# A row softmax over 16384 rows: larger blocks, one broadcast multiply for each, and tiles of twice the size in half as many buffers

## Chip, cores and metric

The kernel runs on one core of one Trainium2 chip. The metric is the device time of one execution in microseconds (us). The median of ten runs of the kernel before is 163.21 us (163.10 to 163.46).

## What is computed

A softmax over the last axis of a float32 tensor of 16 x 1024 x 512, with a temperature of 0.5, so that every element is doubled first:

```python
def reference(x: np.ndarray) -> np.ndarray:
    temp = 0.5
    x_scaled = x / temp
    x_max = np.max(x_scaled, axis=-1, keepdims=True)
    exp_x = np.exp(x_scaled - x_max)
    return (exp_x / np.sum(exp_x, axis=-1, keepdims=True)).astype(np.float32)
```

Input and output are 33.55 MB each. Every byte is read from HBM once and written once.

## The kernel before

The 16384 rows are cut into 8 tiles of 2048 rows. A tile lies on 128 partitions with G = 16 rows of 512 elements each, 32 KiB a partition, and those 16 rows are contiguous in HBM. There are six buffers for tiles, 192 KiB a partition. A tile is transformed in place and stored from where it lies.

A tile is worked on in blocks of B = 4 rows a partition, 32 blocks in all. Five small functions each record one step of a block:

- `shift(i)` on VectorE: the negated maximum of each row (L65, one tensor_reduce for four rows) and its doubling, which is the bias (L67).
- `exponentials(i)` on ScalarE: one activation a row (L74), exp(2x + bias), which also leaves the sum of the row.
- `scale_vector(i)` on VectorE: the reciprocals of the four sums (L87), and three of the four rows multiplied by them, one instruction a row (L89).
- `scale_scalar(i)` on ScalarE: the fourth row multiplied, as a copy with a scale (L95).
- `store(i)` on ScalarE's DMA queue: after the last block of a tile, the whole tile of 4.2 MB (L102).

`load(c)` issues a tile's load on SP's DMA queue (L59). The first tile comes in two pieces, four rows and twelve, the others whole. From the seventh tile on, a load has to wait until the store of the tile six before it has left the buffer.

The order of the instructions on each engine is the order in which the program records them; the schedule is written by hand (`manual_schedule`). The main loop (L105 to L116) is a software pipeline: in step i it records shift and exponentials of block i, then scale_vector of block i-1, scale_scalar of block i-2 and store of block i-3. So on ScalarE the exponentials of block i come ahead of the copy of block i-2. Waits between engines are put in by the framework where data demand them. Each engine, and each DMA queue, works through its own list in order.

Of the kernel before, what the change touches and what calls it, by code (L numbers as in the profile page):

```python
# [1 line left out]

# [4 lines left out]


@with_exitstack
def kernel(  # L10
    ctx: ExitStack,
    tc: tile.TileContext,
    x: bass.AP,
    out: bass.AP,
):
    nc = tc.nc
    fp32 = mybir.dt.float32
    P = nc.NUM_PARTITIONS
    AX = mybir.AxisListType.X
    EXP = mybir.ActivationFunctionType.Exp  # L20
    COPY = mybir.ActivationFunctionType.Copy
    MAX = mybir.AluOpType.max

    D = x.shape[-1]
    xf = x.flatten_outer_dims()
    of = out.flatten_outer_dims()
    N = xf.shape[0]

    G = 16
    B = 4
    N_ACT = 1
    C = N // (P * G)
    assert C * P * G == N
    xr = xf.rearrange("(c p g) d -> c p g d", p=P, g=G)
    outr = of.rearrange("(c p g) d -> c p g d", p=P, g=G)

    FIRST = [(0, 4), (4, 16)]  # L40

    data = ctx.enter_context(tc.tile_pool(name="data", bufs=6))
    stats = ctx.enter_context(tc.tile_pool(name="stats", bufs=6))

    ctx.enter_context(tc.manual_schedule())


    warm = stats.tile([P, 1], fp32, name="warm", bufs=1)
    nc.vector.memset(warm, 0.0)  # L49
    nc.scalar.activation(out=warm, in_=warm, func=EXP)  # L50

    tiles = {}
    blocks = [(c, b) for c in range(C) for b in range(0, G, B)]
    state = {}

    def load(c):
        xt = tiles[c] = data.tile([P, G, D], fp32, name="xt")
        for lo, hi in FIRST if c == 0 else [(0, G)]:
            nc.sync.dma_start(out=xt[:, lo:hi, :], in_=xr[c][:, lo:hi, :])  # L59

    def shift(i):
        c, b = blocks[i]
        xb = tiles[c][:, b : b + B, :]
        negmax = stats.tile([P, B], fp32, name="negmax")
        nc.vector.tensor_reduce(negmax, xb, axis=AX, op=MAX, negate=True)  # L65
        bias = stats.tile([P, B], fp32, name="bias")
        nc.vector.tensor_scalar_mul(bias, negmax, 2.0)  # L67
        state[i] = (xb, bias)

    def exponentials(i):  # L70
        xb, bias = state[i]
        sums = stats.tile([P, B], fp32, name="sums")
        for g in range(B):
            nc.scalar.activation(  # L74
                out=xb[:, g, :],
                in_=xb[:, g, :],
                func=EXP,
                bias=bias[:, g : g + 1],
                scale=2.0,
                accum_out=sums[:, g : g + 1],  # L80
            )
        state[i] = (xb, sums)

    def scale_vector(i):
        xb, sums = state[i]
        recip = stats.tile([P, B], fp32, name="recip")
        nc.vector.reciprocal(recip, sums)  # L87
        for g in range(B - N_ACT):
            nc.vector.tensor_scalar_mul(xb[:, g, :], xb[:, g, :], recip[:, g : g + 1])  # L89
        state[i] = (xb, recip)  # L90

    def scale_scalar(i):
        xb, recip = state[i]
        for g in range(B - N_ACT, B):
            nc.scalar.activation(  # L95
                out=xb[:, g, :], in_=xb[:, g, :], func=COPY, scale=recip[:, g : g + 1]
            )

    def store(i):
        c, b = blocks[i]  # L100
        if b + B == G:
            nc.scalar.dma_start(out=outr[c], in_=tiles[c])  # L102

    n = len(blocks)
    for i in range(n + 3):  # L105
        if i < n:
            if blocks[i][1] == 0:
                load(blocks[i][0])
            shift(i)
            exponentials(i)  # L110
        if 1 <= i <= n:
            scale_vector(i - 1)
        if 2 <= i <= n + 1:
            scale_scalar(i - 2)
        if 3 <= i:
            store(i - 3)  # L116


# [1 line left out]
_INS = ['x']  # L120
_OUTS = [((16, 1024, 512), 'float32')]


# [23 lines left out]
```

## Time and profile before

| | before |
|---|---|
| median of 10 runs | 163.21 us |
| the profiled execution | 163.66 us |
| its span in the profile | 161.6 us |
| VectorE busy | 119.7 us (74%), 193 instructions |
| ScalarE busy | 114.8 us (71%), 290 instructions |
| DMA | 67.14 MB, 416 GB/s over the span |

The span runs from the first instruction of the program to the last; the 2.06 us around it are not in the profile. "Busy" is the time in which an engine executes an instruction. The slices of the profile page cut the span into 40 equal parts of 4.04 us; a digit is the busy share in tenths. In a group of instructions, the numbers behind the bar are the total busy time, the mean duration in ns, and the idle time ahead with what ended it. DVE is VectorE, ACT is ScalarE, SPq and ACTq are the DMA queues of SP and ScalarE. In a view of windows the columns are: length, busy time of VectorE, ScalarE and GpSimd with their counts, the clock of TensorE, the busy share of the DMA engines, and GB/s.

### The profile page before, as it was taken

Reading aid. Unit: us, or ns where it says so; the run is one execution under the profiler, and the core shown is the slowest. Engines: PE = TensorE matmul, PEld = TensorE weight load, DVE = VectorE, ACT = ScalarE, POOL = GpSimd, SP = SyncE. Lnnn points to the kernel's source line nnn. Section 1 sums busy time; section 2 is a strip of 40 time slices with the busy share of each in tenths; the row PEclk is TensorE's granted clock in tenths of the full one; section 3 lists DMA queues with packets and bytes.
Section 4 is the critical chain, followed back from the end, with each engine's and each line's share of the span. In section 5 each row is a group of like instructions: output and inputs, shape, how many; then the busy total and the mean of one; then the engine's idle time right before and its main releaser. Section 6 shows DMA issues by size and latency. Waiting matters only on the chain.

```text
span 161.6 us, 563 instructions
## 1 busy us (share of the span) xinstructions
DVE 119.7 (74%) x193; ACT 114.8 (71%) x290; POOL 0.2 (0%) x4
## 2 busy tenths in 40 slices
DVE  0608999999999999999997999099980999630000
ACT  3071799999999998999996999539993499950000
POOL 0000000000000000000000000000000000000000
DMA  5999999999999999999999999999999999999990
GB/s 185 464 422 487 389 438 470 391 438 341 481 414 406 479 422 397 479 422 397 487 408 397 495 406 389 511 397 389 511 397 389 495 414 391 487 414 406 487 406 24
DMA packets 2452, 67.14 MB, mean 416 GB/s; under 512 B 272, under 2 KB 272, under 8 KB 272
## 3 DMA queue, kind: packets, MB, share of 16 engines
q1 hardware_dynamic: 1296, 33.56, 48.9%
q10 hardware_dynamic: 1152, 33.55, 48.1%
q14 instruction: 4, 0.03, 0.0%
HBM read 33.55 MB, written 33.55 MB: 415 GB/s over the span
## 4 chain that ended last, share of the span: by engine, by line
DMA 54%; DVE 31%; ACT 3%; issue 1%; SPq 0%
DMA xt<-in_x_dram 36%; DVE negmax L65 19%; DMA out_dram<-xt 18%; DVE xt L89 9%; ACT xt L74 2%; DVE bias L67 1%; ACT xt L95 1%; DVE recip L87 1%; SPq L59 0%
## 5 line engine op out<-in xcount | busy, mean ns | idle before, releaser
L74 ACT ACTIVATE xt<-xt,bias 128x512 f32<-128x512 f32 x128 | 90.8, 710 | 28.1 <-DVE bias L67 28.1
L65 DVE TENSOR_REDUCE negmax<-xt 128x4 f32<-128x2048 f32 x32 | 73.0, 2281 | 18.9 <-DMA xt<-in_x_dram 18.9
L89 DVE TENSOR_SCALAR xt<-xt,recip 128x512 f32<-128x512 f32 x96 | 40.9, 483 | 1.1
L74 ACT ACTIVATION_READ_ACCUMULATOR xt<-xt,bias 128x1 f32 x128 | 23.9, 187 | 0.0
L95 ACT ACTIVATE xt<-xt,recip 128x512 f32<-128x512 f32 x32 | 22.4, 706 | 0.0
L87 DVE RECIPROCAL recip<-sums 128x4 f32<-128x4 f32 x32 | 5.5, 171 | 1.6 <-ACT xt L74 1.6
L67 DVE TENSOR_SCALAR bias<-negmax 128x4 f32<-128x4 f32 x32 | 5.4, 170 | 1.1
L50 ACT ACT_TABLE_LOAD x1 | 1.3, 1283 | 0.7 <-PEq L131 0.7
L49 DVE MEMSET warm<- 128x1 f32 x1 | 0.1, 59 | 0.8 <-PEq L131 0.8
L50 ACT ACTIVATE warm<-warm 128x1 f32<-128x1 f32 x1 | 0.2, 202 | 0.0
L131 POOL MEMSET const-bfloat16-1.0<- 128x1 bf16 x1 | 0.1, 101 | 0.0
L131 POOL MEMSET const-uint8-127<- 128x1 uint8 x1 | 0.1, 101 | 0.0
L131 POOL MEMSET const-float32-0.0<- 128x1 f32 x1 | 0.1, 98 | 0.2 <-issue 0.2
L131 POOL MEMSET const-float32-1.0<- 128x1 f32 x1 | 0.1, 98 | 0.0
## 6 DMA issues: line engine op xcount, KB each, us to landing
out_dram<-xt ACTq DMA_DIRECT2D x8, 4096.0 KB, 27.3
xt<-in_x_dram SPq DMA_DIRECT2D x7, 4096.0 KB, 46.4
xt<-in_x_dram SPq DMA_DIRECT2D x1, 3072.0 KB, 11.7
xt<-in_x_dram SPq DMA_DIRECT2D x1, 1024.0 KB, 4.8
```

Source lines behind the costliest of these rows:

```text
L49: nc.vector.memset(warm, 0.0)
L50: nc.scalar.activation(out=warm, in_=warm, func=EXP)
L65: nc.vector.tensor_reduce(negmax, xb, axis=AX, op=MAX, negate=True)
L67: nc.vector.tensor_scalar_mul(bias, negmax, 2.0)
L74: nc.scalar.activation(out=xb[:, g, :], in_=xb[:, g, :], func=EXP, bias=bias[:, g : g + 1], scale=2.0, accum_out=sums[:, g : g + 1],)
L87: nc.vector.reciprocal(recip, sums)
L89: nc.vector.tensor_scalar_mul(xb[:, g, :], xb[:, g, :], recip[:, g : g + 1])
L95: nc.scalar.activation(out=xb[:, g, :], in_=xb[:, g, :], func=COPY, scale=recip[:, g : g + 1])
L131: nc = _bacc.Bacc("TRN2", target_bir_lowering=False, num_devices=1)
```

## The change

Tiles are twice as large: 4 tiles of 32 rows a partition (64 KiB, contiguous in HBM) in three buffers, the same 192 KiB. Loads and stores of the second and third tile are whole, 8.4 MB; those of the first and fourth come in halves of 16 rows, and the first half of the first tile is loaded in three pieces of 1, 3 and 12 rows. The fourth tile takes the first one's buffer by name, half by half.

Blocks are of 4, 4, 8 and 16 rows in the first tile, of 16 rows in the second and third, and of 16, 8 and 8 in the fourth: 11 in all. The three multiplies of a block on VectorE, one a row, become one tensor_mul over three quarters of its rows, with the reciprocals broadcast along the 512 elements. ScalarE still copies the last quarter, one row at a time.

The main loop is another: shift(0), shift(1) and exponentials(0) come ahead; then step i records exponentials of block i+1, scale_vector and scale_scalar of block i, shift of block i+2, and store of block i. So on ScalarE the copies and the store of block i come after the exponentials of block i+1.

The diff, cut to its core (line numbers of the new kernel that the text speaks of: loads L72, maximum L80, doubling L84, exponentials L91, reciprocals L106, multiply L108, copies L117, stores L125):

```diff
-    G = 16
-    B = 4
-    N_ACT = 1
+    G = 32
...
+    WHOLE = [(0, G)]
+    HALVES = [(0, 16), (16, G)]
+    LOADS = [[(0, 1), (1, 4), (4, 16), (16, G)], WHOLE, WHOLE, HALVES]
+    BLOCKS = [
+        [(0, 4), (4, 8), (8, 16), (16, G)],
+        HALVES,
+        HALVES,
+        [(0, 16), (16, 24), (24, G)],
+    ]
+    STORES = [HALVES, WHOLE, WHOLE, HALVES]
+    BMAX = 16
+    BUFS = 3
-    data = ctx.enter_context(tc.tile_pool(name="data", bufs=6))
+    data = ctx.enter_context(tc.tile_pool(name="data", bufs=BUFS))
...
     def load(c):
-        xt = tiles[c] = data.tile([P, G, D], fp32, name="xt")
-        for lo, hi in FIRST if c == 0 else [(0, G)]:
+        if c < BUFS:
+            chunks[c] = data.tile([P, G, D], fp32, name="xt")
+        else:
+            chunks[c] = chunks[c - BUFS]
+        xt = chunks[c]
+        for lo, hi in LOADS[c]:
             nc.sync.dma_start(out=xt[:, lo:hi, :], in_=xr[c][:, lo:hi, :])
...
     def scale_vector(i):
...
-        nc.vector.reciprocal(recip, sums)
-        for g in range(B - N_ACT):
-            nc.vector.tensor_scalar_mul(xb[:, g, :], xb[:, g, :], recip[:, g : g + 1])
+        c, lo, hi = blocks[i]
+        b = hi - lo
+        k = b - b // 4
+        recips[i] = stats.tile([P, BMAX], fp32, name="recip")
+        nc.vector.reciprocal(recips[i][:, 0:b], sums[i][:, 0:b])
+        rows = chunks[c][:, lo : lo + k, :]
+        nc.vector.tensor_mul(
+            rows, rows, recips[i][:, 0:k].unsqueeze(2).broadcast_to((P, k, D))
+        )
...
     def store(i):
-        c, b = blocks[i]
-        if b + B == G:
-            nc.scalar.dma_start(out=outr[c], in_=tiles[c])
+        c, _, end = blocks[i]
+        for lo, hi in STORES[c]:
+            if hi == end:
+                nc.scalar.dma_start(
+                    out=outr[c][:, lo:hi, :], in_=chunks[c][:, lo:hi, :]
+                )
-    for i in range(n + 3):
-        if i < n:
-            if blocks[i][1] == 0:
-                load(blocks[i][0])
-            shift(i)
-            exponentials(i)
-        if 1 <= i <= n:
-            scale_vector(i - 1)
-        if 2 <= i <= n + 1:
-            scale_scalar(i - 2)
-        if 3 <= i:
-            store(i - 3)
+    shift(0)
+    shift(1)
+    exponentials(0)
+    for i in range(n):
+        if i + 1 < n:
+            exponentials(i + 1)
+        scale_vector(i)
+        scale_scalar(i)
+        if i + 2 < n:
+            shift(i + 2)
+        store(i)
```

More of the change, by code (lines that the diff above doesn't have):

```diff
@@ L38 @@
     outr = of.rearrange("(c p g) d -> c p g d", p=P, g=G)
-    FIRST = [(0, 4), (4, 16)]
-    data = ctx.enter_context(tc.tile_pool(name="data", bufs=6))
+    WHOLE = [(0, G)]
[11 more added lines that the diff above has]
+    data = ctx.enter_context(tc.tile_pool(name="data", bufs=BUFS))
     stats = ctx.enter_context(tc.tile_pool(name="stats", bufs=6))
@@ L50 @@
     nc.scalar.activation(out=warm, in_=warm, func=EXP)
-    tiles = {}
-    blocks = [(c, b) for c in range(C) for b in range(0, G, B)]
-    state = {}
+    chunks = {}
+    blocks = [(c, lo, hi) for c in range(C) for lo, hi in BLOCKS[c]]
+    n = len(blocks)
+    biases, sums, recips = {}, {}, {}
     def load(c):
-        xt = tiles[c] = data.tile([P, G, D], fp32, name="xt")
-        for lo, hi in FIRST if c == 0 else [(0, G)]:
+        if c < BUFS:
[4 more added lines that the diff above has]
+        for lo, hi in LOADS[c]:
@@ L59, in load @@
             nc.sync.dma_start(out=xt[:, lo:hi, :], in_=xr[c][:, lo:hi, :])
     def shift(i):
-        c, b = blocks[i]
[L63 to L68, printed above, removed]
+        c, lo, hi = blocks[i]
+        if c not in chunks:
+            load(c)
@@ L70, in exponentials @@
+        b = hi - lo
+        negmax = stats.tile([P, BMAX], fp32, name="negmax")
+        nc.vector.tensor_reduce(
+            negmax[:, 0:b], chunks[c][:, lo:hi, :], axis=AX, op=MAX, negate=True
+        )
+        biases[i] = stats.tile([P, BMAX], fp32, name="bias")
+        nc.vector.tensor_scalar_mul(biases[i][:, 0:b], negmax[:, 0:b], 2.0)
     def exponentials(i):
-        xb, bias = state[i]
-        sums = stats.tile([P, B], fp32, name="sums")
-        for g in range(B):
+        c, lo, hi = blocks[i]
@@ L74, in exponentials @@
+        sums[i] = stats.tile([P, BMAX], fp32, name="sums")
+        for g in range(hi - lo):
+            row = chunks[c][:, lo + g, :]
             nc.scalar.activation(
-                out=xb[:, g, :],
-                in_=xb[:, g, :],
+                out=row,
+                in_=row,
                 func=EXP,
-                bias=bias[:, g : g + 1],
+                bias=biases[i][:, g : g + 1],
                 scale=2.0,
-                accum_out=sums[:, g : g + 1],
+                accum_out=sums[i][:, g : g + 1],
@@ L81, in exponentials @@
             )
-        state[i] = (xb, sums)
     def scale_vector(i):
-        xb, sums = state[i]
-        recip = stats.tile([P, B], fp32, name="recip")
-        nc.vector.reciprocal(recip, sums)
-        for g in range(B - N_ACT):
-            nc.vector.tensor_scalar_mul(xb[:, g, :], xb[:, g, :], recip[:, g : g + 1])
-        state[i] = (xb, recip)
+        c, lo, hi = blocks[i]
+        b = hi - lo
+        k = b - b // 4
+        recips[i] = stats.tile([P, BMAX], fp32, name="recip")
+        nc.vector.reciprocal(recips[i][:, 0:b], sums[i][:, 0:b])
@@ L92, in scale_scalar @@
+        rows = chunks[c][:, lo : lo + k, :]
+        nc.vector.tensor_mul(
+            rows, rows, recips[i][:, 0:k].unsqueeze(2).broadcast_to((P, k, D))
+        )
     def scale_scalar(i):
-        xb, recip = state[i]
-        for g in range(B - N_ACT, B):
+        c, lo, hi = blocks[i]
+        b = hi - lo
+        for g in range(b - b // 4, b):
+            row = chunks[c][:, lo + g, :]
             nc.scalar.activation(
-                out=xb[:, g, :], in_=xb[:, g, :], func=COPY, scale=recip[:, g : g + 1]
+                out=row, in_=row, func=COPY, scale=recips[i][:, g : g + 1]
@@ L97, in scale_scalar @@
             )
     def store(i):
-        c, b = blocks[i]
-        if b + B == G:
-            nc.scalar.dma_start(out=outr[c], in_=tiles[c])
-    n = len(blocks)
-    for i in range(n + 3):
-        if i < n:
-            if blocks[i][1] == 0:
-                load(blocks[i][0])
-            shift(i)
-            exponentials(i)
-        if 1 <= i <= n:
-            scale_vector(i - 1)
-        if 2 <= i <= n + 1:
-            scale_scalar(i - 2)
-        if 3 <= i:
-            store(i - 3)
+        c, _, end = blocks[i]
@@ L120 @@
+        for lo, hi in STORES[c]:
+            if hi == end:
+                nc.scalar.dma_start(
+                    out=outr[c][:, lo:hi, :], in_=chunks[c][:, lo:hi, :]
+                )
+    shift(0)
[9 more added lines that the diff above has]
+        store(i)
 _INS = ['x']
```

## The prediction

> **What bounds the kernel now.** I read the page's forty slices first, then the windows, then the groups, then the order of time on VectorE and ScalarE. The page says where the limit is:
>
> ```profile
> DVE  0608999999999999999997999099980999630000
> ACT  3071799999999998999996999539993499950000
> DMA  5999999999999999999999999999999999999990
> q1 hardware_dynamic: 1296, 33.56, 48.9%
> q10 hardware_dynamic: 1152, 33.55, 48.1%
> ```
>
> The DMA engines are busy from the first slice to the last but one; loads (q1) and stores (q10) together fill 97.0% of the span. VectorE and ScalarE have holes, so they are not the limit. The windows view gives the rate (last column, GB/s; the column before it is the busy share):
>
> ```profile
> 13.00:36.00 23.00, 22.58 (x37) 18.77 (x49) 0.00 (x0) 1.00 1.00 433
> 36.00:41.00 5.00, 4.93 (x7) 4.75 (x14) 0.00 (x0) 1.00 1.07 406
> 144.00:156.00 12.00, 0.00 (x0) 0.00 (x0) 0.00 (x0) 1.00 1.01 434
> 156.00:158.00 2.00, 0.00 (x0) 0.00 (x0) 0.00 (x0) 1.00 0.68 295
> 158.00:161.60 3.60, 0.00 (x0) 0.00 (x0) 0.00 (x0) 1.00 0.04 18
> ```
>
> Loads alone (13 to 36 us) and stores alone (144 to 156) run at 433 and 434 GB/s. 67.11 MB at 433 take 155.0 us; the rest of the 161.6 us is the start, some loss where the first store joins, and a tail from about 157 us in which a few DMA engines finish late. So whatever leaves the DMA queues empty in mid-run is added to the time, and nothing that VectorE saves is gained as long as they are full. How far the kernel is from emptying them: the timeline has the last store's issue, and its forerunner's:
>
> ```profile
> 135.08 0.34 ACTq L102 DMA_DIRECT2D out_dram<-xt  x1
> ...
> 143.63 0.34 ACTq L102 DMA_DIRECT2D out_dram<-xt  x1
> ```
>
> From 143.6 to about 158 the queue moves 14.4 us x 433 GB/s = 6.2 MB, of which the last store is 4.2 MB; so 2.0 MB of the store before it was still waiting: about 4.7 us of cover. The compute chain stays ahead of the stores by that little. The costs of the chain, from the page's groups and from one block of VectorE in order of time:
>
> ```profile
> L74 ACT ACTIVATE xt<-xt,bias 128x512 f32<-128x512 f32 x128 | 90.8, 710 | 28.1 <-DVE bias L67 28.1
> L65 DVE TENSOR_REDUCE negmax<-xt 128x4 f32<-128x2048 f32 x32 | 73.0, 2281 | 18.9 <-DMA xt<-in_x_dram 18.9
> L89 DVE TENSOR_SCALAR xt<-xt,recip 128x512 f32<-128x512 f32 x96 | 40.9, 483 | 1.1
> ```
> ```profile
> 128.73 2.28 DVE L65 TENSOR_REDUCE negmax<-xt 128x4 f32<-128x2048 f32 x1
> 131.04 0.17 DVE L67 TENSOR_SCALAR bias<-negmax 128x4 f32<-128x4 f32 x1
> 131.12 0.17 DVE L87 RECIPROCAL recip<-sums 128x4 f32<-128x4 f32 x1
> 131.33 1.28 DVE L89 TENSOR_SCALAR xt<-xt,recip 128x512 f32<-128x512 f32 x3
> 132.52 2.28 DVE L65 TENSOR_REDUCE negmax<-xt 128x4 f32<-128x2048 f32 x1
> ```
>
> Maximum to maximum is 3.79 us for four rows, 15.2 us for sixteen. Three scalings take 1.28 us, 0.427 us each. On ScalarE four exponentials run from 131.25 to 134.09, where the next operation starts: 0.71 us each (0.705 between starts), and three copies in a row take 1.93 us, so 0.61 us for each further one.
>
> [...] with both queues full (41 to 124 us) the sum is 430 GB/s, not more than for one alone.
>
> **The change, part by part.**
> 1. Bigger blocks. 32 blocks of 4 become 11: two of 4 rows, three of 8, six of 16. Maxima: 32 instructions become 11 over the same 65536 elements[...]. Doublings and reciprocals: 21 of each less, 0.08 and 0.21 us each on the path by the rows above, 6.1 us. Sum on VectorE: -9.2 us.
> 2. One tensor_mul with the reciprocals broadcast replaces the scalings by row (L89). Not in the trace. From the nearest row, 12 rows at 0.427 = 5.12 us[...]. I take 6.56[...], and keep the others for rivals. [...] With part 1, VectorE ends about 3 us heavier; a 16-row block costs 8.68 (maximum[...]) + 0.03 + 0.08 + 0.21 + 6.56 - 0.09 (the overlap with the next maximum, as in the rows above) = 15.47 us, for 15.2 before. Alone this would be hidden.
> 3. Tiles of 8.4 MB. The same 192 KiB a partition, but the middle tiles are loaded and stored whole. The second tile is not usable until 16.8 MB have landed. In the trace 4.2 MB have landed at 12.85 (where the second block's maximum starts); the other 12.6 MB at 433 GB/s need 29.1 us, so 41.9. VectorE has then been waiting from about 36 us, where the first tile's two halves have had their maxima.
> 4. Stores. Before, a store of 4.2 MB went out about every 15.2 us, and ScalarE's queue reached it several blocks after its data. Now store(i) comes straight after scale_scalar(i), but that comes after exponentials(i+1) of a whole 16-row block in ScalarE's queue. The wait of the store for VectorE's multiply holds the next exponentials, which wait for VectorE's next maximum anyway: nothing more.
> 5. Row pieces of 64 KiB in place of 32. The two queues show what pieces could matter: the loads have 144 packets more and 0.8% of the span, 1.3 us, more, most of it at the start. I take 0, bounds -0.5 and +0.5. One piece more at the start (first row alone): the first block still waits for row 3; 0 to +0.1.
> 6. Three buffers for six half-size ones: each half of the fourth tile waits at L72 for the store of the first tile's half. On SP nothing is queued behind but the other half. The fourth tile's halves should land at about 92 and 104 us by equal sharing, and are needed at 104 and 121: hidden.
>
> Now the path to the third tile's store. From 41.9: four blocks at 15.47 = 61.9, to 103.8; then the maximum of the fourth tile's first block and its doubling, 8.68 + 0.23, to 112.7; its 16 exponentials on ScalarE, 16 x 0.705 + 0.1 = 11.4, to 124.1; then the four copies of the third tile's last block, 2.5, to 126.6; store issued. (The multiply of that block, 112.9 to 119.5, is ready before.) First bytes about 1.0 us later, as at the start, where SP issues at 0.73 and the first packets show at about 1.7: 127.6.
>
> What has the DMA to do until then? All loads (33.55 MB), and stores of the first two tiles (16.78): all but 16.78 MB. Before, everything is moved at about 158.0; less 16.78 MB / 433 = 38.8 us gives 119.2. So the engines stand idle from 119.2 to 127.6: **8.4 us**. The third tile's store and the two last halves then run on without a hole: issued at about 135 and 145, needed at 147 and 156. Given back: the late DMA engines catch up in the hole; their tail (last bytes about 2 us after the others, the window 156 to 160) should shrink by some 1.5 us, estimated, since it grew over the whole run and now starts anew with 40 us left. Parts 5: 0 to -0.3; I take -0.2.
>
> Sum: 161.6 + 8.4 - 1.5 - 0.2 = 168.3 us of span. The profiled execution took 163.66, 2.06 more than its span, and lies 0.45 above the median 163.21. The difference of 6.7 us put on the median: **169.9 us**.
>
> **Rivals.** *The broadcast multiply is cheap.* The path holds four multiplies of 12 rows, so it moves by four times their error. The hole is gone, and with it the loss, when one takes 4.9 us or less (8.4 - 1.5 - 0.2 = 6.7; 6.7/4 = 1.7 below 6.56). [...] from 50.8 five times (11.4 + 2.5) = 69.5, store at 120.3, first bytes 121.3, a hole of 2.1 and 1.7 given back: 163.6 at most, 163.2 if the tail shrinks a little more. Not slower within what can be told. [...] Nothing beats it by much, since the DMA moves the same bytes.
>
> *The third tile lands late.* It is needed at 41.9 + 2 x 15.47 = 72.8. The first half tile's store goes out at about 45 (its chain has the same rows). Shared evenly from then on, the 4.2 MB of store and the 7.0 MB of load left (25.17 less 41.9 us' 16.78 and 3.1 us x 433) end at 45 + 11.2/0.433 = 71 to 73: just in time. If the queues take turns by pieces, 64 KiB against 32, it is sooner. Should stores get two thirds, it is about 80: +7 us of path, 177. For it: the margin is small. Against: both queues moved equal bytes in near equal shares (48.9 and 48.1%).
>
> *The broadcast multiply is slow*[...].
>
> *The change doesn't do what it says*: the saving of instructions is real, but on an engine that isn't the limit; that is in the forecast already.
>
> **How the numbers follow.** The forecast has 80 in 100: the multiply at 6.2 to 6.9 us (4 x 0.35 = 1.4 each way), restart of the queue 0.6 to 2 us, tail and pieces -0.7 to +1.5: 167.4 to 173.0. The cheap multiply has 12 (163 to 166.5), the late tile 5 (up to 177), the slow multiply 3. The range, 165.5 to 173.0, takes in 2 of the 12 and 2 of the 5; left out are 10 + 3 + 3, and 2 of the forecast's edges. What can be told from no change here is 0.2%, 0.33 us. Faster comes only from the cheap multiply with a tail or pieces better than thought: 4. Within 0.2%: 4, from the same case. Slower: 92, the 4 left of it and all others.
>
> **What would show it.** In the profile after: the L108 row (12 rows) at about 6.5 us mean; the slices of DMA full but for a hole of two slices around 119 to 128 us; the third tile's store issued at about 127; VectorE waiting for DMA at about 36 to 42 us and hardly later. The prediction is wrong if DMA shows no hole, if L108 lies below 4.9 us, or if VectorE waits for loads after 60 us.

## The result and the profile after

| | before | after |
|---|---|---|
| median | 163.18 us (28 runs) | 170.5 us (8 runs, 170.19 to 170.66) |
| span of the profiled execution | 161.6 us | 168.6 us |
| VectorE busy | 119.7 us | 125.7 us |
| ScalarE busy | 114.8 us | 112.5 us |
| mean DMA rate over the span | 416 GB/s | 398 GB/s |

The change makes the kernel slower: the ratio is 1.0444, with a 95% interval from 1.0434 to 1.0454. Forecast were 169.9 us and a span of 168.3. Ratios, here and below, are taken against the kernel before, run beside each kernel, and leave out runs over 1.5% above the fastest of their own kernel; there were two of four such runs with the loads in halves and 13 of 20 in the copy with large pieces, whose medians so stand above their ratios.

The page of the changed kernel, the same slices as before (each is now 4.2 us):

```profile
DVE  0509999950999999999999999999999994600000
ACT  3063486299608995999599879959998999300000
DMA  5998999699988999999999999979705999598985
GB/s 190 449 480 381 490 498 498 264 484 498 482 249 358 420 451 428 435 404 466 396 466 373 396 342 461 498 311 466 311 0 249 498 498 498 249 498 373 498 373 249
q1 hardware_dynamic: 1152, 33.55, 48.3%
q10 hardware_dynamic: 864, 33.55, 46.1%
```

In the DMA row there is now a slice of 0, the thirtieth (122.2 to 126.5 us): with half of the stores still to do, no packet begins. Before, no slice between the first and the last was below 9. VectorE and ScalarE are full in that very slice, so the DMA engines wait for them and not the other way about. The windows view narrows the hole (columns as before: VectorE, ScalarE, GpSimd, clock, DMA share, GB/s):

```profile
46.00:54.00 8.00, 7.93 (x4) 2.62 (x7) 0.00 (x0) 1.00 1.08 401
90.00:103.00 13.00, 12.93 (x4) 11.28 (x31) 0.00 (x0) 1.00 1.05 393
121.00:123.00 2.00, 2.00 (x1) 2.00 (x7) 0.00 (x0) 1.00 0.15 66
123.00:125.00 2.00, 1.80 (x2) 2.00 (x7) 0.00 (x0) 1.00 0.00 0
125.00:127.00 2.00, 1.96 (x2) 2.00 (x4) 0.00 (x0) 1.00 0.00 0
...
127.00:128.20 1.20, 1.20 (x1) 0.73 (x2) 0.00 (x0) 1.00 0.00 0
128.20:128.80 0.60, 0.60 (x1) 0.60 (x3) 0.00 (x0) 1.00 4.09 1745
```

A packet is one piece of a transfer as a DMA engine moves it, here for the most part one partition's 32 or 64 KiB (512 and 256 of the 864 packets of the changed kernel's store queue). The view books a packet whole in the window in which it begins; a short window shows more than 433 GB/s where many begin in it. So read these rows as the times at which packets begin. The last ones before the hole begin soon after 121, the first ones after it between 128.2 and 128.8 (1745 GB/s x 0.6 us = 1.05 MB, one packet of 64 KiB for each of the 16 engines, at 4.09 x 0.6 = 2.45 us each): no packet begins for about 7 us. Since the last ones still run for 2.4 us, the engines' idle time is less. Worked out from the trace's packet records, each packet followed over its whole length, it is 6.4 us, the mean of the 16 engines between 120 and 130.

Two weaker stretches lie ahead of it, 401 GB/s from 46 to 54 us and 393 from 90 to 103. There the engines are hardly idle, but their packets take longer. By the same records they move 368 and 365 GB/s; against 433 that costs 1.2 and 2.0 us. The page agrees: the two queues fill 94.4% of 168.6 us, which is 159.2, where before they filled 97.0% of 161.6, which is 156.8. Of the 7.0 us by which the span grew, 2.4 are the same bytes taking longer, and 4.6 are idle time.

Why the hole ends at 128: VectorE's and ScalarE's order of time about there, and the store.

```profile
104.67 8.68 DVE L80 TENSOR_REDUCE negmax<-xt 128x16 f32<-128x8192 f32 x1
113.38 0.17 DVE L84 TENSOR_SCALAR bias<-negmax 128x16 f32<-128x16 f32 x1
113.46 0.24 DVE L106 RECIPROCAL recip<-sums 128x16 f32<-128x16 f32 x1
113.74 6.56 DVE L108 TENSOR_TENSOR xt<-xt,recip 128x6144 f32<-128x6144 f32 x1
```
```profile
113.59 0.72 ACT L91 ACTIVATE xt<-xt,bias 128x512 f32<-128x512 f32 x1 [1.71 <-DVE bias L84]
...
124.18 0.71 ACT L91 ACTIVATE xt<-xt,bias 128x512 f32<-128x512 f32 x1
124.79 0.19 ACT L91 ACTIVATION_READ_ACCUMULATOR xt<-xt,bias 128x1 f32 x1
124.88 2.55 ACT L117 ACTIVATE xt<-xt,recip 128x512 f32<-128x512 f32 x4
127.46 0.34 ACTq L125 DMA_DIRECT2D out_dram<-xt  x1
```

VectorE has scaled the third tile's last rows at 120.3. The reciprocals for ScalarE's four rows are there at 113.7. But ScalarE first does the next block's 16 exponentials, 113.59 to 124.88, then the four copies, 2.55 us, and the store of the whole 8.4 MB goes out at 127.46. Forecast was 126.6.

The groups that were priced, by shape:

```profile
L80 DVE TENSOR_REDUCE negmax<-xt 128x16 f32<-128x8192 f32 x6 | 52.1, 8679 | 6.5 <-DMA xt<-in_x_dram 6.5
L108 DVE TENSOR_TENSOR xt<-xt,recip 128x6144 f32<-128x6144 f32 x6 | 39.3, 6558 | 0.2
```

The maximum of 16 rows takes 8679 ns (forecast 8.68 us), the broadcast multiply of 12 rows 6558 (6.56). The 6.5 us of idle time ahead of the maxima is the one wait for the second tile, which ends at 42.45; VectorE waits for no load after it.

The end of the run. Ahead, the changed kernel; below it the kernel before:

```profile
166.00:166.30 0.30, 0.00 (x0) 0.00 (x0) 0.00 (x0) 1.00 2.03 874
166.30:168.60 2.30, 0.00 (x0) 0.00 (x0) 0.00 (x0) 1.00 0.00 0
```
```profile
157.00:158.00 1.00, 0.00 (x0) 0.00 (x0) 0.00 (x0) 1.00 0.46 197
158.00:161.60 3.60, 0.00 (x0) 0.00 (x0) 0.00 (x0) 1.00 0.04 18
```

After the hole, no packet begins later than 166.3, 2.3 us ahead of the span's end. Before, 18 GB/s x 3.6 us = 65 KB, two packets of 32 KiB, begin in the last 3.6 us: stragglers. After the hole all engines start again together, and none is left behind; this is what the forecast gave back as 1.5 us.

### The profile page after: what moved, and what is told of

It is laid out like the page before. It is cut to its first block, busy times and chain, and to the rows that moved or that the text cites. A ratio compares the mean times of both kernels' runs of the same rounds, so it can differ in the third digit from the quotient of the medians.

```text
span 168.6 us, 414 instructions
## 1 busy us (share of the span) xinstructions
DVE 125.7 (75%) x45; ACT 112.5 (67%) x290; POOL 0.2 (0%) x4
## 4 chain that ended last, share of the span: by engine, by line
DVE 51%; DMA 24%; ACT 10%; SPq 1%; issue 1%
DVE negmax L80 28%; DMA xt<-in_x_dram 24%; DVE xt L108 21%; ACT xt L91 10%; SPq L72 1%; DVE recip L106 1%; DVE bias L84 1%
## 5 line engine op out<-in xcount | busy, mean ns | idle before, releaser
L91 ACT ACTIVATE xt<-xt,bias 128x512 f32<-128x512 f32 x128 | 90.4, 708 | 31.5 <-DVE bias L84 30.6
L80 DVE TENSOR_REDUCE negmax<-xt 128x16 f32<-128x8192 f32 (+2 forms) x11 | 69.9, 6353 | 16.0 <-DMA xt<-in_x_dram 16.0
L108 DVE TENSOR_TENSOR xt<-xt,recip 128x6144 f32<-128x6144 f32 (+2 forms) x11 | 52.9, 4812 | 0.4
L91 ACT ACTIVATION_READ_ACCUMULATOR xt<-xt,bias 128x1 f32 x128 | 24.0, 187 | 0.0
L117 ACT ACTIVATE xt<-xt,recip 128x512 f32<-128x512 f32 x32 | 20.5, 707 | 0.0
L106 DVE RECIPROCAL recip<-sums 128x16 f32<-128x16 f32 (+2 forms) x11 | 2.4, 220 | 2.6 <-ACT xt L91 2.6
L84 DVE TENSOR_SCALAR bias<-negmax 128x16 f32<-128x16 f32 (+2 forms) x11 | 1.9, 173 | 0.4
```

The lines of the kernel that those rows point to most:

```text
L80: nc.vector.tensor_reduce(negmax[:, 0:b], chunks[c][:, lo:hi, :], axis=AX, op=MAX, negate=True)
L84: nc.vector.tensor_scalar_mul(biases[i][:, 0:b], negmax[:, 0:b], 2.0)
L91: nc.scalar.activation(out=row, in_=row, func=EXP, bias=biases[i][:, g : g + 1], scale=2.0, accum_out=sums[i][:, g : g + 1],)
L106: nc.vector.reciprocal(recips[i][:, 0:b], sums[i][:, 0:b])
L108: nc.vector.tensor_mul(rows, rows, recips[i][:, 0:k].unsqueeze(2).broadcast_to((P, k, D)))
L117: nc.scalar.activation(out=row, in_=row, func=COPY, scale=recips[i][:, g : g + 1])
```

## Experiments

All but the two copies change only the place named; the rest is the changed kernel. Its median is 170.5.

**Third and second tile stored in halves.**

```diff
-    STORES = [HALVES, WHOLE, WHOLE, HALVES]
+    STORES = [HALVES, HALVES, HALVES, HALVES]
```

> The changed kernel with one thing undone: the second and third tile are stored in halves of 4.2 MB, each as soon as its block is scaled (loads stay whole). Theory (the DMA engines stand idle because the whole third tile's store is issued only at 127.5 us): the third tile's first half goes out about 14 us sooner, at 112 to 113, its 9.7 us of bytes cover the hole, and the time falls to 162.5 to 164.5 us. Rival (the time is lost in the DMA engines, by 64 KiB pieces or fewer transfers in flight): half of the 64 KiB pieces go, so about half of the loss, 166 to 168 us. Rival (VectorE's heavier multiply sets the end): 170 to 171, unchanged, since VectorE's work is the same.

Measured: 163.46 us, ratio to the kernel before 1.0013 (0.9999 to 1.0027). With one list changed, the time is the kernel before's again, to within 0.3%. The third tile's halves go out at 112.0 and 127.6; in the place of the hole its windows have:

```profile
119.00:127.00 8.00, 7.76 (x5) 8.00 (x22) 0.00 (x0) 1.00 1.01 434
```

VectorE's work is the same 125.7 us as in the changed kernel, so the heavier multiply is no loss by itself.

**Only the second tile, and only the third, stored in halves.**

```diff
-    STORES = [HALVES, WHOLE, WHOLE, HALVES]
+    STORES = [HALVES, HALVES, WHOLE, HALVES]
```

> The changed kernel with only the second tile stored in halves (the third stays whole). Its first half goes out at 81 in place of 96 us, so the DMA engines have work between 90 and 103 us, where they ran at 393 GB/s. Theory (what counts is when the third tile's store is issued, 127.5, and that does not move): the work done sooner only makes the hole after it longer, from 119 to 128 us; 170 to 171 us, unchanged. Rival (each place where DMA falls below 433 GB/s costs by itself): 168.5 to 169.5.

Measured: 170.14 us, 1.0425 (1.0407 to 1.0442), an interval that overlaps the changed kernel's (1.0434 to 1.0454). The weak stretch from 90 to 103 is gone, and the hole begins sooner:

```profile
90.00:103.00 13.00, 12.93 (x4) 11.28 (x31) 0.00 (x0) 1.00 1.01 437
...
119.00:121.00 2.00, 2.00 (x2) 2.00 (x7) 0.00 (x0) 1.00 0.23 98
121.00:123.00 2.00, 2.00 (x1) 2.00 (x7) 0.00 (x0) 1.00 0.00 0
```

437 for 393 GB/s from 90 to 103; but packets cease to begin between 119 and 121, where the changed kernel went on until after 121. The store is issued at 127.26 as before. Bytes moved sooner are worth nothing while a later store sets the end.

```diff
-    STORES = [HALVES, WHOLE, WHOLE, HALVES]
+    STORES = [HALVES, WHOLE, HALVES, HALVES]
```

> The changed kernel with only the third tile stored in halves (the second stays whole). Its first half goes out at 112 us. Theory: the hole at 121 is gone, and what remains of the loss is the weak stretch from 90 to 103 us (1.2 us) and the one at 46 to 54, which both stay: 164.3 to 165.6 us, above the kernel with both halved (163.46) by about what the second tile's late store costs. Rival (the remainder seen with the copies moved came from moving them, not from the second tile's store): 163 to 163.8.

Measured: 165.13 us, 1.0117 (1.0081 to 1.0152). The hole is gone (369 GB/s from 119 to 127 by the packets that begin there; followed over their length, they keep all engines busy), the weak stretch stays (401 from 90 to 103). The third tile alone is 5.4 us of the 7.0; the second tile's late store is worth the remaining 1.7, but only once the third no longer hides it.

**Rows scaled one by one.**

```diff
-        nc.vector.tensor_mul(
-            rows, rows, recips[i][:, 0:k].unsqueeze(2).broadcast_to((P, k, D))
-        )
+        for g in range(k):
+            nc.vector.tensor_scalar_mul(
+                rows[:, g, :], rows[:, g, :], recips[i][:, g : g + 1]
+            )
```

> The changed kernel with one thing undone: VectorE multiplies its rows one by one again (12 scalings of 0.427 us in place of one multiply of 6.56), tiles, stores and order as changed. Theory: four such multiplies lie on the path to the third tile's store, so it is issued 4 x 1.4 = 5.7 us sooner, at about 122, and the hole shrinks from 7.2 to about 1.7 us; the late DMA engines then have less to catch up in; 164.7 to 166.5 us. Rival (64 KiB pieces): unchanged, 170 to 171. Rival (only the late second tile matters): unchanged.

Measured: 164.49 us, 1.0076 (1.0051 to 1.0100), 0.2 us below the lower end. Pieces of 64 KiB, tiles and order are untouched, so the pieces can't be the cause of more than the 1.3 us that are left (164.49 against 163.15 beside it). The groups view, and the third tile's store:

```profile
L109 DVE TENSOR_SCALAR xt<-xt,recip 128x512 f32<-128x512 f32 x96 | 39.0, 482 | 0.4
```
```profile
121.48 0.34 ACTq L126 DMA_DIRECT2D out_dram<-xt  x1
```

The store is 6.0 us sooner (5.7 expected) and the time 6.0 us shorter: one for one. Here the multiply costs just what it adds to the path. Twelve scalings of a block that stand in one row take 4.84 us, so 0.40 each, somewhat less than the 0.427 that came from three.

**Loads in halves.**

```diff
-    LOADS = [[(0, 1), (1, 4), (4, 16), (16, G)], WHOLE, WHOLE, HALVES]
+    LOADS = [[(0, 1), (1, 4), (4, 16), (16, G)], HALVES, HALVES, HALVES]
```

> The changed kernel with one thing undone: the second and third tile are loaded in halves (stores stay whole). Theory: VectorE no longer waits from 36 to 42.4 us for the whole second tile, so the path to the third tile's store starts 6.4 us sooner and the store is issued at about 121; the hole closes to about 1 us; 164 to 166 us, if the third tile's first half lands by about 67. If that half lands late the gain is smaller, 166 to 168. Rival (64 KiB pieces): loads no longer have them, half of the loss goes, 166 to 168, and then the hole stays where it is. Rival (whole stores as such): unchanged, 170 to 171.

Measured: 1.0095 (1.0066 to 1.0123), which is 164.7 us against 163.15 beside it. The median of its four runs is 166.2, just above the range expected, so the size of the gain is less sure here than in the other kernels. VectorE starts on the second tile at 35.8 in place of 42.45 and the store goes out at 120.80, as forecast. In VectorE's order of time a new wait shows, which was not forecast:

```profile
121.35 4.42 DVE L80 TENSOR_REDUCE negmax<-xt 128x8 f32<-128x4096 f32 x1 [7.70 <-DMA xt<-in_x_dram]
```

The fourth tile's second half lands late, since its load (q1) shares the engines with the second tile's whole store (q10). The DMA view from 96 to 116 us shows how they share:

```profile
q10 hardware_dynamic: 84, 5.51, 63.5%
q1 hardware_dynamic: 85, 2.79, 32.2%
```

The packets are equal in number, 84 and 85, not in bytes: in this stretch the queues took turns packet by packet, so that the store, in packets of 64 KiB, moved twice what the load did in packets of 32 (5.51 MB to 2.79). VectorE, being early, waits 7.7 us. The wait begins at 113.65, behind VectorE's share of the third tile, and leaves that tile's store where it is.

**Copies ahead of the exponentials, for one block.**

```diff
-        if i + 1 < n:
+        if i + 1 < n and i != 7:
             exponentials(i + 1)
         scale_vector(i)
         scale_scalar(i)
+        if i == 7:
+            exponentials(i + 1)
...
-                nc.scalar.dma_start(
+                (nc.sync if i == 7 else nc.scalar).dma_start(
```

> The changed kernel with only the order at one place changed: ScalarE makes the four copies of the third tile's last block ahead of the 16 exponentials of the next block, and the third tile's store is issued from SP's queue, whose loads are all out by 90 us, so that it waits for its data alone. Pieces, sizes and instructions are the same. Theory: the store is issued when VectorE's multiply ends, at about 120.3, 7 us sooner; the hole at 121 is gone or below 1 us; 163.5 to 165.5 us. Rivals (64 KiB pieces; heavier multiply; late second tile): unchanged, 170 to 171.

Measured: 165.38 us, 1.0123 (1.0101 to 1.0145).

```profile
120.28 0.35 SPq L125 DMA_DIRECT2D out_dram<-xt  x1
```

The store goes out when VectorE's multiply ends, 7.2 us sooner, with every size, piece and instruction as in the changed kernel; beside the order, only the queue that issues this store is another. The time falls by 5.1. What is left agrees with the kernel that has only its third tile halved (165.13): the weak stretch from 90 to 103 stays in both (393 and 401 GB/s).

**All transfers in halves: the block part of the change alone.**

```diff
-    LOADS = [[(0, 1), (1, 4), (4, 16), (16, G)], WHOLE, WHOLE, HALVES]
+    LOADS = [[(0, 1), (1, 4), (4, 16), (16, G)], HALVES, HALVES, HALVES]
...
-    STORES = [HALVES, WHOLE, WHOLE, HALVES]
+    STORES = [HALVES, HALVES, HALVES, HALVES]
```

> The block part of the change alone: the second and third tile are loaded and stored in halves, so that every transfer is one of the kernel before or smaller; blocks of up to 16 rows, the broadcast multiply and the new order stay. Theory (blocks and multiply cost VectorE some us but nothing in time as long as the stores come in time): no hole, 162.7 to 163.8 us, the same as the kernel before within 0.4%. Rival (the bigger blocks and the multiply alone cost part of the loss, because a store of a half tile still waits behind 16 exponentials of the next block): 165 to 168 us.

Measured: 162.58 us, 0.9957 (0.9941 to 0.9973): 0.4% below the kernel before, 0.1 us under the range expected, and the shortest of the kernels here that compute. Its page:

```profile
DVE  0507999999999999999999999999799994800000
ACT  3071759089989989995999599959998979600000
DMA  5999999999999999999999999999999999999993
q1 hardware_dynamic: 1440, 33.56, 49.5%
q10 hardware_dynamic: 1152, 33.55, 48.4%
```

The DMA row is full, at 97.9% for the two queues (97.0 before). So the larger blocks, the broadcast multiply and the new order are harmless with transfers of half a tile; the loss needs the whole ones. It isn't theirs alone: with whole transfers kept, cheaper rows or another order take back 5 to 6 of the 7 us. It arises where a store of a whole tile stands at the end of a path that is too long.

**Loads and stores without computation.** Two kernels in which the functions for VectorE and ScalarE are not called and each store waits for its load alone:

```diff
-    shift(0)
...
-        store(i)
+    for c in range(C):
+        load(c)
+        for lo, hi in STORES[c]:
+            nc.scalar.dma_start(
+                out=outr[c][:, lo:hi, :], in_=chunks[c][:, lo:hi, :]
+            )
```

> The changed kernel's loads and stores without any computation: all maxima, exponentials and multiplies are left out, the output is the input, and each store waits only for its load. Pieces of 64 KiB in the second and third tile. Theory (pieces cost nothing by themselves): within 0.6 us of the same kernel with 32 KiB pieces, both 160 to 163.5 us, near the kernel before. Rival (64 KiB pieces are slow): 2 us or more above the one with 32 KiB.

> As the copy with 64 KiB pieces, all computation left out and the output is the input, but all tiles go in halves, 32 KiB pieces. Theory: 160 to 163.5 us; this is the least that the 67 MB take in this form, and it is within 2 us of the kernel before. Rival (the kernel before is bound by its engines): 155 us or less.

Measured: 32 KiB pieces 162.21 us, 0.9931 (0.9903 to 0.9958); 64 KiB pieces 0.9985 (0.9952 to 1.0019), with single runs from 161.4 to 167.8 and a median of 164.1. The copy with small pieces is only 1.0 us below the kernel before and 0.4 below the best kernel: this kernel's floor in this form is the transfer itself. By the ratios the large pieces cost 0.9 us more (0.0054 x 163.2), by the medians of all runs 1.9; expected were at most 0.6, and both between 160 and 163.5; the rival said 2 or more. So this pair doesn't rule out a cost of the large pieces of that size, and why their times spread so far was not settled. Pieces and whole transfers change together in it. In the changed kernel they matter little, by the runs above that keep them: with rows one by one, all but 1.3 us of the loss is gone.

## Why the prediction was right, and which terms were off

**What bounds the kernel** was read rightly: the DMA engines. The copy without computation takes 162.21 us where the whole kernel takes 163.2.

**Instructions saved on VectorE, and the multiply's price** (parts 1 and 2): VectorE is 6.0 us heavier (125.7 for 119.7), forecast 3. The groups come out near the forecast: on the two pages VectorE's four groups sum to 124.8 us before and 127.1 after, 2.3 more. The maxima fall from 73.0 to 69.9, doublings and reciprocals from 10.9 to 4.3, and the multiplies rise from 40.9 to 52.9. But "busy" counts an overlap of two instructions once, and the 32 short blocks overlapped by 5.2 us in all, the 11 long ones by 1.5. The forecast counted only a part of this where it summed what fewer blocks save. It did no harm, since the time was worked out from the block of 16 rows, forecast 15.47 us, measured 15.55 (from one maximum's start to the next, 58.01 to 73.56). Two terms of that block were not shown by the trace of the kernel before, which has maxima of 4 rows at 2281 ns and no multiply of two tensors: 8.68 us for the maximum of 16 rows, where 8679 ns are measured, and 6.56 us for the multiply of 12 rows with its broadcast operand, where 6558 ns are measured. The forecast's loss rests largely on the second: at 0.427 us a row, which the trace before had, the path to the third tile's store would be 4 x 1.44 = 5.8 us shorter. The rivals with a cheap or a slow multiply fall by these 6558 ns. The forecast's threshold for the cheap one was too high: at 4.9 us or less no loss should be left, but the rows one by one, at 4.84 us, leave 1.3.

**The late start** (part 3): 41.9 forecast, 42.45 measured. **The third tile lands late**, the second rival, falls: VectorE shows no wait for it when it takes it up at 73.56. The margin was about 3 us: with the rows one by one VectorE is there earlier and waits for this tile until 70.42. What the forecast left open, whether the queues share evenly or take turns by pieces, is settled for one stretch by the DMA view of the changed kernel from 54 to 66 us: 48 packets of the load, 3.15 MB, to 50 of the store, 1.64 MB. Turns by pieces favoured this load.

**The order on ScalarE** (part 4): right, with the store at 127.46 for 126.6; 0.55 us of the 0.86 are the later start and four times 0.08 the blocks.

**The hole**: right in what it costs, off in its parts. Forecast was one hole of 8.4 us from 119.2. Measured are 6.4 us of idle time between 120 and 130, and 3.2 us lost ahead of it (46 to 54 and 90 to 103), where the kernel before lost 0.7 us at its own first store (36 to 41): 8.9 us. The forecast had taken the DMA engines to move 433 GB/s up to the hole. The kernel with only its second tile halved shows that the two are one account: without the stretch from 90 to 103, the hole begins sooner and the time stays.

**Given back at the end**: 1.5 us by forecast, 1.8 measured. The kernel before loses 3.2 us of transfer time after 150 us, the changed kernel 1.4 after 160, since its last packets end together. 8.9 less 1.8 is 7.1, for 7.0 by which the span grew. Part of these 1.8 us may belong to the one profiled execution of the kernel before, which lies 0.48 us above the median.

**Why the sum came so close**: what sets the end is the issue of the third tile's store, and 16.8 MB that are still to be moved after it: 127.46 + 0.9 to its first packets + 38.8 = 167.2, and the last packets, which begin by 166.3 and take 1.2 us, end about there. This mechanism is the forecast's. By its own numbers the bytes end at 126.6 + 1.0 + 38.8 = 166.4, 1.9 us ahead of the span's end; measured are 167.2 and 1.4. Two errors of opposite sign, 0.8 and 0.5 us, leave the 0.3 by which the span was missed: that the forecast came so close is in part luck, the mechanism is not.

**That the loss has this cause** is shown from three sides, all without touching VectorE's instructions or without touching the pieces: sooner by halves (112.0), by cheaper rows (121.48), by order alone (120.28). The time followed the third tile's store each time, up to the point where the store no longer sets the end: 6.0 us for 6.0 with cheaper rows, 5.1 for 7.2 by order, where the weak stretches remain. Why the best kernel is 0.6 us below the kernel before is open. Its trace shows where the time goes: it loses 2.1 us after 150 us, the kernel before 3.2; what makes the stragglers fewer was not tried.

## What to carry to other kernels

When transfers bound a kernel, count bytes against time: from a store's issue back, what has the DMA still in its queue? A store in one piece can't start before its last row is done, so doubling its size moves its start by half a tile's compute (127.5 in place of 112.0 here), and cover of 4.7 us was not enough for that. Look also at what stands ahead of a store in the issuing engine's list: sixteen exponentials of the next block held back the third tile by 7 us. And an engine with idle time on average (VectorE at 75%) can still be the path to one store that decides.

## What was not expected of the hardware

A store issued while only loads were in flight had no packet begin for some 4 us (45.10 to 49.44), and the rate fell meanwhile (368 GB/s from 46 to 54, for 433). In the changed kernel the first store is issued at 45.10; the DMA view from 45.1 to 49.3 us shows packets of the load queue alone, and up to 50.0 the first two of the store queue:

```profile
q1 hardware_dynamic: 30, 1.97, 133.1%
```
```profile
q1 hardware_dynamic: 30, 1.97, 114.1%
q10 hardware_dynamic: 2, 0.07, 3.1%
```

A share above 100% is no error: each packet is booked where it begins. 133.1% of 16 engines' 4.2 us are 89 us for 30 packets, 3.0 us each, where 64 KiB at 433 GB/s over 16 engines take 2.42. So the load's packets take longer while the store starts. The store at 127.46, with both queues empty, had its first packets at 128.2 to 128.8.

The same is seen at the second tile's store, issued at 96.35: its first packet begins after 100.5, and 1.4 us of transfer time are lost from 96 to 104. In the kernel with the second tile halved, a store issued at 96.14, while the store queue is still at work, costs nothing (437 GB/s from 90 to 103). And the copy with small pieces, which computes nothing and issues its first store at 13.66, moves 413 GB/s from 13 to 36, where both kernels that compute move 433, with a slice of 278 from 16.0 to 20.1. So in these runs the fall goes with a store that starts on an idle queue beside busy loads, and not with the computing engines. What causes it was not tried, nor what makes up the rest of the stretch from 90 to 103, 0.5 us from 90 to 93.5, ahead of that store.
